# Longer rows for the slots of activations and split weights in a two-layer hybrid backbone kernel

## The chip, the core and the metric

The kernel runs on one core of one Trainium2 chip. The metric is device time in microseconds (us) from one launch, as the median of several executions. The times of the kernel before are 1237.31 us in the median of three (1236.67 to 1237.4). The profile shows one further execution, taken by the hardware profiler.

## The reference

Two consecutive layers (one gated-DeltaNet mixer, one HGRN2 mixer, each followed by a squared-ReLU MLP) are applied to 128 context tokens and 256 latent tokens that share one set of weights, with a model width of 1024. Cut to what matters for the time:

```python
for layer in range(2):
    sh1, sc1, gt1, sh2, sc2, gt2 = split(silu(c) @ w_ada[layer] + b_ada[layer], 6)
    h = rms_norm(x, g0) * (1 + sc1) + sh1
    mix = gated_deltanet(h) if layer == 0 else hgrn2(h)    # projections 1024 -> 4128 or 5120, back to 1024
    x = x + gt1 * rms_norm(mix, g1)
    h = rms_norm(x, g2) * (1 + sc2) + sh2
    x = x + gt2 * rms_norm(square(relu(h @ w1[layer])) @ w2[layer], g3)    # 1024 -> 4096 -> 1024
```

Everything is float32. The outputs are the 384 rows of x and the final states of both mixers.

## The kernel before

The 384 tokens are kept as three tiles of 128. All weights stream once from HBM. To multiply float32 numbers at one pass per matmul, each operand is split into a high and a low part of type fp32r: `hi` is a cast of the value (ScalarE), `lo` is value minus `hi` (VectorE), and a product becomes three matmuls, hi·hi, hi·lo and lo·hi (`mm3`). For weights, `split` makes the tiles `wh` and `wl` from a raw tile `wr` that a DMA has filled. For activations the split tiles are `hhi` and `hlo` (normalised input, transposed), and `mh` and `ml` (the hidden layer of the MLP).

A matmul with output `pj`, `k` or `nat` multiplies weights by `hhi`/`hlo`; `acc` is the output of the two down projections; `pf` holds the HGRN2 gate and value projections. In the names of the profile, the output stands first, then the moving operand (streamed, one column after the other) and the stationary one (loaded into the array by a LDWEIGHTS ahead of it), or the same two in the program's order.

All work tiles live in one pool that is divided into classes of equal slots, and a tile takes any free slot of its class. The classes that matter here:

- `L6`, 11 slots of 128 partitions by 6144 bytes (1536 float32): `hhi`, `hlo`, `mh`, `ml`, `xn`, `sg`, `hk`, `lhl`, and the Gated-DeltaNet tiles `PU`, `kT`, `T64`
- `wh` and `wl`, three slots each, 4096 bytes per partition
- `L1` (17 slots: `mr`, `cacc`, `cb`, `qT`, `CR` and others), `L3`, `L4` (`av`, `ar`, `hE`, `HC`, `x`), `Lh`, and `wr` (two slots of 8192 bytes)

In the program as it is built, the first byte of a slot within its partition, modulo 256, is called its phase here. Before the change every slot of `L6`, `wh` and `wl` has phase 96, since their rows are multiples of 256 bytes. `wr`, `L3`, `L4` and `Lh` have phase 224. The slots of `L1` are 1600 bytes apart and have phases 160, 224, 32 and 96 in turn. The constants have phases of their own (`sml` 128, `cst` 96). Within a tile, the pieces that a matmul reads begin at multiples of 512 bytes, so they keep the phase of the slot.

A planner (`Planner.run`) decides the order of all instructions and the slots from costs in a table; it doesn't look at addresses. `Planner.tile` registers a tile with its shape (L614 of the kernel before), `Planner.run` takes the real tile from the pool when its first instruction is issued (L798), and `fix` (L507) turns an access pattern of the planner into one of the real tile.

Of the kernel before, what the change touches and what calls it, by code (L numbers as in the profile page):

```python
# [10 lines left out]
B16 = mybir.dt.bfloat16  # L11
# [334 lines left out]
 'z:ld': 12621,  # L346
 'z:sp': 10349}
ZS = 2
DRY = False
V_KINDS = ((0, "gt2"), (1, "sh1"), (1, "sc1"), (1, "gt1"), (1, "sh2"), (1, "sc2"), (1, "gt2"))  # L350
ADA_KINDS = ("sh1", "sc1", "gt1", "sh2", "sc2", "gt2")
# [103 lines left out]
class VAP:  # L455
    def __init__(self, tensor, offset, ap, dtype, space):
        self.tensor, self.offset, self.ap, self.dtype, self.space = tensor, offset, ap, dtype, space
# [42 lines left out]


class VTile:
    def __init__(self, name):
        self.name, self.real = name, None


def fix(x):  # L507
    if isinstance(x, VAP):
        return bass.AP(tensor=x.tensor.real.tensor, offset=x.offset, ap=[list(d) for d in x.ap])
    return x  # L510


# [27 lines left out]
class Planner:  # L540
# [71 lines left out]
        return op  # L612

    def tile(self, pool, shape, dtype, cls, tag, bufs, space=None):  # L614
        t = VTile(f"{tag}_{len(self.tile_of)}")
        bufs = BUFS.get(tag, bufs)
        ap, st = [], 1
        for n in reversed(shape):
            ap.append((st, n))
            st *= n  # L620
        self.tile_of[t.name] = {"cls": cls, "tag": tag, "bufs": bufs, "first": None, "left": 0, "got": False, "name": t.name,
                                "make": (pool, shape, dtype), "v": t}
        return VAP(t, 0, ap[::-1], dtype, space)

    def run(self):
# [163 lines left out]
        self.plan = done  # L789
        if DRY:  # L790
            return
# [28 lines left out]
class Vec:  # L820
# [14 lines left out]
    def tensor_tensor(self, out, in0, in1, op):  # L835
        rate = 1.042 if self.e == "V" else (164.0 if op == ALU.pow else 2.1)
        base = None if self.e == "V" else (300.0 if op == ALU.pow else 150.0)
        self._go(lambda: self.r.tensor_tensor(fix(out), fix(in0), fix(in1), op), _n(out), [out], [in0, in1], rate, base=base)  # L838

    def scalar_tensor_tensor(self, out, in0, scalar, in1, op0, op1, accum_out=None):  # L840
        w = [out] if accum_out is None else [out, accum_out]
        kw = {} if accum_out is None else {"accum_out": accum_out}
        self._go(lambda: self.r.scalar_tensor_tensor(fix(out), fix(in0), fix(scalar), fix(in1), op0, op1, **{k: fix(v) for k, v in kw.items()}), _n(out), w,  # L843
                 [in0, scalar, in1], 1.042, extra=62.0 * (accum_out is not None), scal=(scalar,))

    def tensor_scalar(self, out, in0, s1, s2, op0, op1=None):
        rate = (0.521 if self._fast(out, in0) else 1.042) if self.e == "V" else 1.042
        args = (out, in0, s1, s2, op0) if op1 is None else (out, in0, s1, s2, op0, op1)
        self._go(lambda: self.r.tensor_scalar(*[fix(x) for x in args]), _n(out), [out], [in0, s1, s2], rate, base=None if self.e == "V" else 160.0, scal=(s1, s2))  # L849
# [95 lines left out]
def kernel(ctx: ExitStack, tc: tile.TileContext, a, o):  # L945
# [12 lines left out]
    def tl(cls, tag, bufs, shape, dtype=F):  # L958
        return pl.tile(pool, shape, dtype, cls, tag, bufs)
# [366 lines left out]
    def zgate(p):  # L1326
        t = tl("L1", "th", 2, [128, T])
        S.activation(t, p, AF.Tanh, scale=0.5)
        zs = tl("L1", "zs", ZS, [128, T])
        V.scalar_tensor_tensor(zs, t, 1.0, p, ALU.add, ALU.mult)  # L1330
# [14 lines left out]
    def gdn(oT):  # L1345
# [136 lines left out]
        def gate(h, p):  # L1482
            pl.unit(f"z{h}")
            zs = tl("L1", "zs", ZS, [128, T])
            S.activation(zs, p, AF.Silu)
# [599 lines left out]
```

## Time and profile before

| What | Value |
|---|---|
| median of 3 executions | 1237.31 us (1236.67 to 1237.4) |
| profiled execution, its own time | 1235.33 us |
| span of its trace, first to last instruction | 1233.3 us |
| mean granted TensorE clock, share of full speed | 0.966 |
| TensorE busy (PE) | 1180.0 us, 96% of the span |
| weight loads (PEld), beside the matmuls | 1047.6 us, 85% |
| VectorE busy (DVE) | 800.2 us, 65% |
| ScalarE busy (ACT) | 635.4 us, 52% |
| GpSimd busy (POOL) | 66.1 us, 5% |

PE's busy time is a union of intervals whose ends are modelled; one matmul's own duration overlaps the next one. What a matmul costs in a stream is therefore the time from one start to the next, which a merged piece of the chain of waits gives when it is divided by its count.

### The profile page before, as it was taken

The numbers are of one execution on the slowest core, as the hardware profiler recorded it, in microseconds if no ns is written. First come the engines' busy times: TensorE is split into PE (matmuls) and PEld (weight loads), VectorE is DVE, ScalarE is ACT, GpSimd is POOL, SyncE is SP. The second block draws the span as 40 slices with busy tenths as digits, with TensorE's granted clock in tenths as the row PEclk, the third lists the DMA queues.
The fourth block names the chain that finished last, engine by engine and source line by source line (L and its number), as shares of the span: only waits on it lengthen the run. The fifth ranks groups of instructions, "written<-read, shape, count | busy, mean of one in ns | idle before, by whom it ended". The sixth has DMA issues, their size and how long they took to land.

```text
span 1233.3 us, 20383 instructions
## 1 busy us (share of the span) xinstructions
PE 1180.0 (96%) x7936; PEld 1047.6 (85%) x7936; DVE 800.2 (65%) x1578; ACT 635.4 (52%) x1283; POOL 66.1 (5%) x156
## 2 busy tenths in 40 slices
PE   6998998999998999999998999999998999999997
PEld 3775988888987998989988998888986999888986
DVE  4484878867999986666539967767666542333334
ACT  3383464775646643343436567674655564333442
POOL 1111001000002000000002000000002000000000
PEclk9996996899998999999998999999999999999999
DMA  9868771675353875556436642233432334233432
GB/s 359 318 248 281 225 214 33 198 248 186 119 182 134 302 237 191 192 184 205 152 115 205 210 150 97 76 110 111 159 133 84 107 137 137 103 127 118 138 129 86
DMA packets 82642, 207.82 MB, mean 169 GB/s; under 512 B 26058, under 2 KB 47842, under 8 KB 70514
## 3 DMA queue, kind: packets, MB, share of 16 engines
q1 hardware_dynamic: 82546, 206.53, 49.4%
q8 instruction: 62, 1.02, 0.3%
q14 instruction: 34, 0.28, 0.1%
HBM read 192.52 MB, written 13.99 MB: 167 GB/s over the span
## 4 chain that ended last, share of the span: by engine, by line
PE 60%; DVE 7%; ACT 5%; issue 2%; POOL 1%; POOLq 0%; DVEq 0%; ACTq 0%
PE acc L924 24%; PE pj L924 21%; PE pf L924 7%; PE nat L924 3%; PE pb L924 2%; PE po L924 1%; DVE wl L838 1%; ACT L887 1%; DVE A L838 1%; POOL rstd L838 1%; PE pb L930 1%; PE pj L930 1%; ACT wh L892 1%; DVE avj L843 1%; DVE hQD L838 1%
## 5 line engine op out<-in xcount | busy, mean ns | idle before, releaser
L838 DVE TENSOR_TENSOR wl<-wr,wh 128x1024 fp32r<-128x1024 f32 (+2 forms) x228 | 266.6, 1171 | 268.1 <-ACT wh L892 260.1
L892 ACT CAST wh<-wr 128x1024 fp32r<-128x1024 f32 (+2 forms) x228 | 230.3, 1010 | 403.8 <-PE pj L924 178.0
L924 PE MATMUL pj<-hhi,wh 128*128 128x384 f32 x800 | 272.5, 343 | 0.0
L924 PE MATMUL pj<-hhi,wl 128*128 128x384 f32 x800 | 271.1, 342 | 0.0
L924 PE MATMUL pj<-hlo,wh 128*128 128x384 f32 x800 | 270.9, 341 | 0.0
L924 PEld LDWEIGHTS pj<-hhi,wh 128*128 128x128 f32 x800 | 151.6, 190 | 2.4 <-issue 0.8
L924 PEld LDWEIGHTS pj<-hlo,wh 128*128 128x128 f32 x800 | 151.5, 190 | 1.8 <-issue 0.4
L924 PEld LDWEIGHTS pj<-hhi,wl 128*128 128x128 f32 x800 | 151.6, 190 | 1.4 <-DVE wl L838 0.5
L924 PE MATMUL acc<-wl,mh 128*128 128x512 f32 x384 | 149.5, 390 | 0.0
L924 PE MATMUL acc<-wh,ml 128*128 128x512 f32 x384 | 149.3, 390 | 0.0
L924 PE MATMUL acc<-wh,mh 128*128 128x512 f32 x384 | 145.4, 390 | 0.0
L843 DVE SCALAR_TENSOR_TENSOR avj<-av,cvec 128x1024 bf16<-128x1024 f32 x112 | 135.5, 1218 | 6.9 <-DMA dd<-dec 3.7
L924 PEld LDWEIGHTS acc<-wl,mh 128*128 128x128 f32 x384 | 72.1, 188 | 15.8
L924 PEld LDWEIGHTS acc<-wh,mh 128*128 128x128 f32 x384 | 72.1, 188 | 14.7
L924 PEld LDWEIGHTS acc<-wh,ml 128*128 128x128 f32 x384 | 72.1, 188 | 14.2
L924 PE MATMUL pf<-wh,hhi 128*128 128x384 f32 x192 | 63.6, 346 | 2.3 <-ACT hhi L892 2.3
L924 PE MATMUL pf<-wl,hhi 128*128 128x384 f32 x192 | 63.9, 342 | 0.1
L924 PE MATMUL pf<-wh,hlo 128*128 128x384 f32 x192 | 63.8, 345 | 0.0
L843 DVE SCALAR_TENSOR_TENSOR cacc<-cb,sml,cacc 128x392 f32<-128x392 f32 x96 | 58.9, 619 | 5.4 <-ACT cacc L887 4.5
L887 ACT ACT_TABLE_LOAD x35 | 44.9, 1283 | 3.6 <-DVE hk L849 2.4
L838 DVE TENSOR_TENSOR ml<-mr,mh 128x384 fp32r<-128x384 f32 x56 | 30.2, 554 | 14.7 <-PE acc L924 7.5
L924 PEld LDWEIGHTS pf<-wh,hhi 128*128 128x128 f32 x192 | 36.2, 190 | 2.9 <-ACT hhi L892 2.5
(255 smaller groups left out, 1898.0 us busy)
## 6 DMA issues: line engine op xcount, KB each, us to landing
wr<-in_w_dram SPq DMA_DIRECT2D x64, 1024.0 KB
av<-in_wv_dram SPq DMA_DIRECT2D x56, 512.0 KB
ar<-in_wa_dram SPq DMA_DIRECT2D x40, 512.0 KB
wr<-in_gq_dram SPq DMA_DIRECT2D x14, 1024.0 KB
wr<-in_hfi_dram SPq DMA_DIRECT2D x16, 768.0 KB
wr<-in_hqz_dram SPq DMA_DIRECT2D x8, 1024.0 KB
wr<-in_gout_dram SPq DMA_DIRECT2D x4, 1024.0 KB
wr<-in_hout_dram SPq DMA_DIRECT2D x4, 1024.0 KB
```

The source lines that it names most:

```text
L838: self._go(lambda: self.r.tensor_tensor(fix(out), fix(in0), fix(in1), op), _n(out), [out], [in0, in1], rate, base=base)
L843: self._go(lambda: self.r.scalar_tensor_tensor(fix(out), fix(in0), fix(scalar), fix(in1), op0, op1, **{k: fix(v) for k, v in kw.items()}), ...
L887: self.pl.add("S", lambda: self.r.activation(fix(out), fix(in_), func, **{k: fix(v) for k, v in kw.items()}), cost, w, [x for x in (in_, b ...
L892: self.pl.add("S", lambda: self.r.copy(fix(out), fix(in_)), cost, [out], [in_])
L924: self.pl.add("PE", lambda: self.r.matmul(fix(out), lhsT=fix(lhsT), rhs=fix(rhs), start=start() if callable(start) else start, stop=stop, ...
L930: self.pl.add("PE", lambda: self.r.transpose(fix(out), fix(in_), fix(ident)), 111.0, [out], [in_, ident], geo=(4, 4))
```

## The change

Tiles of class `L6` now take slots of 1544 float32 (6176 bytes) and those of `wh` and `wl` slots of 1040 (4160 bytes). The tile in it is as large as before, and only the distance between slots grows, by 32 and by 64 bytes. `fix` puts the longer row into the partition step of the access pattern.

```diff
+ROW = {'L6': 1536 + 8, 'wh': 1024 + 16, 'wl': 1024 + 16}
...
 def fix(x):
     if isinstance(x, VAP):
-        return bass.AP(tensor=x.tensor.real.tensor, offset=x.offset, ap=[list(d) for d in x.ap])
+        t = x.tensor
+        p, f = divmod(x.offset, t.row)
+        dims = [list(d) for d in x.ap]
+        if t.wide != t.row:
+            assert dims[0][0] % t.row == 0
+            dims[0][0] = dims[0][0] // t.row * t.wide
+        return bass.AP(tensor=t.real.tensor, offset=p * t.wide + f, ap=dims)
     return x
...
     def tile(self, pool, shape, dtype, cls, tag, bufs, space=None):
-        t = VTile(f"{tag}_{len(self.tile_of)}")
+        row = 1
+        for n in shape[1:]:
+            row *= n
+        wide = ROW[cls] if cls in ROW and dtype != B16 else row
+        t = VTile(f"{tag}_{len(self.tile_of)}", row, wide)
+        if wide != row:
+            real_shape = [shape[0], wide]
+        else:
+            real_shape = shape
...
-                                "make": (pool, shape, dtype), "v": t}
+                                "make": (pool, real_shape, dtype), "v": t}
```

In the two programs as they are built, all five engines have the same instructions in the same order with the same waits; they differ in addresses alone. The phases after the change are 224, 0, 32, 64, 96, 128, 160, 192, 224, 0 and 32 for the eleven slots of `L6`, 192, 0 and 64 for `wh`, and 128, 192 and 0 for `wl`. `L1`, `L3`, `L4`, `Lh` and `wr` stay where they were. Each tile is in the slot of the same number as before. Instructions with at least one operand in a slot of `L6`, `wh` or `wl`: 5416 of 6676 matmuls of the program, 461 of ScalarE, 446 of VectorE, 4 of GpSimd, and 24 DMAs. The partition needs 736 bytes more and holds them.

## Rows read from the trace of the kernel before

**Rows 1.** The page: busy time of each engine.
```profile
PE 1180.0 (96%) x7936; PEld 1047.6 (85%) x7936; DVE 800.2 (65%) x1578; ACT 635.4 (52%) x1283; POOL 66.1 (5%) x156
```

**Rows 2.** The page: shares of the chain of waits, by engine.
```profile
PE 60%; DVE 7%; ACT 5%; issue 2%; POOL 1%; POOLq 0%; DVEq 0%; ACTq 0%
```

**Rows 3.** Busy time of each engine in five stretches.
```profile
core 0: us, PE busy (x) PEld busy (x) DVE busy (x) ACT busy (x) POOL busy (x), PEclk, DMA share, GB/s
0.00:300.00 300.00, 271.77 (x2270) 228.57 (x2270) 208.63 (x537) 164.42 (x394) 25.83 (x75) 0.90 0.70 232
300.00:421.00 121.00, 115.41 (x722) 106.26 (x722) 112.53 (x224) 72.42 (x188) 12.19 (x27) 0.97 0.50 175
421.00:649.00 228.00, 228.00 (x1141) 205.77 (x1141) 143.59 (x196) 95.72 (x138) 1.10 (x4) 1.00 0.56 188
```

**Rows 4.** The chain from 420 to 650 us: start, length, what.
```profile
420.81 33.31 PE pj L924 x192
454.12 32.68 PE acc L924 x144
486.80 16.66 PE pj L924 x96
...
618.86 31.26 PE acc L924 x138
```

**Rows 5.** Groups of PE by shape: one of each triple, and a load.
```profile
L924 PE MATMUL pj<-hhi,wh 128*128 128x384 f32 x800 | 272.5, 343 | 0.0
...
L924 PE MATMUL acc<-wh,mh 128*128 128x512 f32 x384 | 145.4, 390 | 0.0
...
L924 PE MATMUL pf<-wh,hhi 128*128 128x384 f32 x192 | 63.6, 346 | 2.3 <-ACT hhi L892 2.3
...
L924 PE MATMUL acc<-wh,hhi 128*128 128x512 f32 x96 | 38.0, 406 | 0.2 <-ACT hhi L892 0.2
...
L924 PE MATMUL nat<-wh,hhi 128*128 128x256 f32 x96 | 26.8, 292 | 3.4 <-ACT hhi L892 3.4
...
L924 PE MATMUL k<-hhi,wh 128*128 128x384 f32 x40 | 13.2, 361 | 0.2 <-ACT hhi L892 0.2
```

**Rows 6.** The timeline of PE at 785 us: start, length, what.
```profile
785.49 0.52 PE L924 MATMUL pb<-lhl,CR 128*128 128x256 f32 x3
785.84 1.31 PE L924 MATMUL pb<-HC,lhl 128*128 128x512 f32 x5
```

**Rows 7.** The timeline of PE at 454 us, first and eighth matmul of a piece.
```profile
453.96 0.39 PE L924 MATMUL acc<-wh,mh 128*128 128x512 f32 x1
...
455.57 0.40 PE L924 MATMUL acc<-wl,mh 128*128 128x512 f32 x1
```

**Rows 8.** The chain from 390 to 420 us, one piece.
```profile
395.81 5.67 PE nat L924 x47
```

**Rows 9.** Groups of DVE by shape: busy and mean ns, idle time before.
```profile
L838 DVE TENSOR_TENSOR wl<-wr,wh 128x1024 fp32r<-128x1024 f32 x188 | 229.7, 1223 | 252.3 <-ACT wh L892 244.4 <-PE pj L924 4.7
L843 DVE SCALAR_TENSOR_TENSOR cacc<-cb,sml,cacc 128x392 f32<-128x392 f32 x96 | 58.9, 619 | 5.4 <-ACT cacc L887 4.5
```

**Rows 10.** Tile mr on DVE, 420 to 660 us: minimum, median, maximum ns.
```profile
L838 DVE TENSOR_TENSOR ml<-mr,mh x25: 548/553/559, 422.4 to 621.3; 128x384 fp32r<-128x384 f32 x25
```

**Rows 11.** Groups of ACT by shape: busy and mean ns, idle time before.
```profile
L892 ACT CAST wh<-wr 128x1024 fp32r<-128x1024 f32 x188 | 197.7, 1051 | 354.2 <-PE pj L924 167.0 <-PE acc L924 166.2 <-PE pf L924 15.0
L892 ACT CAST mh<-mr 128x384 fp32r<-128x384 f32 x56 | 27.6, 512 | 1.2
```

**Rows 12.** DMA issues that touch L6: count and size of one.
```profile
du<-PU SPq DMA_DIRECT2D x8, 48.0 KB
...
T<-dt SPq DMA_DIRECT2D x8, 48.0 KB
PU<-dt SPq DMA_DIRECT2D x8, 48.0 KB
```

**Rows 13.** Tile T, 150 to 330 us: issue times of its DMAs.
```profile
L941 SPq DMA_DIRECT2D T<-dt x8: 422/468/5198, 169.3 to 234.3; - x8
```

More of the change, by code (lines that the diff above doesn't have):

```diff
@@ L502, with __init__ @@
 class VTile:
-    def __init__(self, name):
-        self.name, self.real = name, None
+    def __init__(self, name, row, wide):
+        self.name, self.real, self.row, self.wide = name, None, row, wide
 def fix(x):
     if isinstance(x, VAP):
-        return bass.AP(tensor=x.tensor.real.tensor, offset=x.offset, ap=[list(d) for d in x.ap])
+        t = x.tensor
[5 more added lines that the diff above has]
+        return bass.AP(tensor=t.real.tensor, offset=p * t.wide + f, ap=dims)
     return x
```

## The prediction

> **What bounds the kernel now.** I read the busy times first. TensorE is busy for 96% of the span, and no other engine comes near it [rows 1]. The chain of waits says the same with less weight: 60% of it is TensorE, 7% VectorE, 5% ScalarE [rows 2]. So the question is whether TensorE streams at its best rate or loses something that an address could give back or take away.
>
> The stretches answer where to look: from 421 to 649 us (the MLP of the first layer) TensorE is busy all the time, the granted clock is 1.00, and nothing else is near its limit [rows 3]. In that stretch the chain is nothing but matmuls [rows 4]. The piece of 192 matmuls of 384 columns takes 33.31 us, 173.5 ns from one start to the next. The piece of 144 with 512 columns takes 32.68 us, 226.9 ns. [...] What is left is 13 ns in both (173.5 - 384 x 0.417 and 226.9 - 512 x 0.417). The piece of 47 with 256 columns gives 120.6 ns, and again about 14 ns are left [rows 8]. So a matmul in a stream costs its columns at full clock and a constant of some 13 ns. All of these have both operands in slots of phase 96, the one case that the change removes. [...]
>
> **The change part by part.** No instruction, wait or order changes, so the sum has one term for each kind of access.
>
> *Matmuls.* The groups that read two re-placed slots hold 3 x (800 + 384 + 192 + 96 + 96 + 40) = 4824 matmuls [rows 5]. The bound on a gain is the whole constant, 4824 x 13.1 ns = 63 us. For the value itself I use the places where the trace of before already has unequal phases. In the HGRN2 stage a matmul streams `HC` (phase 224) while weights from `lhl` (phase 96) are loaded for the next one: five of 512 columns take 1.31 us, and with the last one's 0.39 us taken off, as in the group beside it, (1.31 - 0.39) / 4 = 230 ns [rows 6, 7]. Three of 256 columns that stream `lhl` (96) against weights in `CR` (160) start within 0.35 us of the next piece, 117 ns each [rows 6]. With 64 or 128 bytes between the phases the constant is thus still 10 to 16 ns. The other bound comes from the same rows: 230 is 3.1 ns more than 226.9, and 4824 x 3.1 ns = 15 us of loss. But matmuls with equal phases take 230 ns too when they come right after another shape: the eight from 453.96 to 455.57 us stand (455.57 - 453.96) / 7 = 230 ns apart [rows 7]. So I take 0, nearest to these rows, between -63 and +15 us.
>
> [...] Each matmul here has a weight load of its own, and no run here shows a stream without them.
>
> *VectorE and ScalarE.* The trace has these engines at many phases. The 25 subtractions `ml<-mr,mh` of the first MLP take 548 to 559 ns [rows 10], while `mr` sat in slots of phase 96 six times, 224 nine times, 32 eight times and 160 twice, and `mh` always at 96. So equal and unequal phases of the two inputs lie within 1%. The four taps of the convolution read `cb` shifted by 4, 8, 12 and 16 bytes against a `cacc` that stays, and have a mean of 619 ns over 96 instructions [rows 9]; 392 elements cost what 384 and 8 more would. The largest groups in re-placed slots are the subtraction into `wl` (229.7 us) and the casts into `wh` and `mh` (197.7 and 27.6 us) [rows 9, 11]. A change of 1% of the two engines' share is 4.6 us of busy time; only 12% of the chain is theirs [rows 2], which leaves about 0.5 us either way. I take 0.
>
> *DMAs.* Of 24 DMAs of 48 KB each, 8 read from `PU`, 8 write `T64` and 8 write `PU` [rows 12], all in pieces of 128 bytes. The issues of the 8 into `T64` have a median of 468 ns and a minimum of 422 ns [rows 13]. If an address shifted each by that difference, it would be 24 x 46 ns = 1.1 us either way, in a stretch in which TensorE still has other work for 272 of 300 us [rows 3]. I take 0. The large transfers go to `wr`, `L3` and `L4`, which don't move.
>
> The sum is 0. The profiled execution's own time is 1235.33 us (span 1233.3 us and 2.0 us around it), so its time after is 1235.3 us; it stands 2.0 us below the median of 1237.31, and so I predict 1237.3 us for the median.
>
> **The rivals.** *A: the constant is a collision.* The stream of one matmul and the weight load of the next walk through the same phase, the load takes cycles from the stream, and slots at unequal phases end that. For it speaks that loads are busy for 85% of the span beside the matmuls [rows 1]; against it that the constant is there at phase distances of 64 and 128 [rows 6]. About a tenth of the pairs would still meet at equal phases, so up to 57 us go; where TensorE is not the chain less arrives, at 60% [rows 2] 34 us. The time would be 1180 to 1203 us, and I name 1190 us. It decides from 0.5 ns per matmul (0.5 x 4824 = 2.4 us).
>
> *B, slower: unequal phases cost the stream.* If the 230 ns of `HC` are due to its phase and not to the change of shape, the 15 us come on top, 1252 us. It has the same point from which it decides, 0.5 ns. For it is the 230 against 226.9; against it are the equal phases with the same 230 [rows 7].
>
> *C: the clock.* Nothing that TensorE does changes by the sum, but a stretch at lower granted clock may come or go when events shift by nanoseconds. From 300 to 421 us the clock is 0.97 [rows 3]; one such loss is 0.03 x 121 = 3.6 us, to either side: 1233.7 or 1240.9 us.
>
> **How the numbers follow.** No change has 0.84, A 0.06, B 0.05, C 0.05, half to each side. About 0.2%, 2.5 us, is what a measurement can tell from no change. Faster by over 0.2% is A and half of C, 0.085; slower is B and half of C, 0.075; within it 0.84. The range needs only the first case: 1237.3 us with 1.6 us for the DMAs and the two engines and 1.7 us of the 2.0 us by which single executions of before stood apart, 1234.0 to 1240.6 us.
>
> **What would show it.** In the profile after, pieces of 384 columns should still come to 173.5 ns and of 512 to 226.9 ns, the group into `wl` to 1223 ns and the cast into `wh` to 1051 ns. A shows as a piece of 192 that takes well under 33.31 us, B as one that takes over 33.5 us. If these stay and the time moves, the granted clock or the DMAs of the inverse should show why. I am wrong if a phase distance that before doesn't have (32 bytes, or slots at a multiple of 64) behaves unlike those it has: in before nearly all slots are at odd multiples of 32, and so the trace can't exclude it.

## The result, and the profile after

| | before | after |
|---|---|---|
| median of four executions | 1236.99 us (1236.06 to 1237.4) | 1243.95 us (1243.58 to 1244.44) |
| profiled execution, its own time | 1235.33 us | 1243.92 us |
| span of its trace | 1233.3 us | 1242.0 us |
| mean granted TensorE clock | 0.966 | 0.967 |

The ratio is 1.0058 with an interval of [1.004, 1.0075]: slower by 0.6%, 3.35 us above the upper end of the predicted range. What comes next shows the kernel after, in which the same code stands 15 lines further down (the matmul's L924 is L939).

The page, busy time of each engine, stands against [rows 1]: PE has 10.5 us more for the same 7936 instructions, VectorE 0.9 us more, ScalarE 0.4 us.

```profile
PE 1190.5 (96%) x7936; PEld 1051.6 (85%) x7936; DVE 801.1 (65%) x1578; ACT 635.8 (51%) x1283; POOL 66.7 (5%) x156
```

The shares of the chain by engine are nearly those of [rows 2], so no new wait has come to the front.

```profile
PE 60%; DVE 7%; ACT 6%; issue 2%; POOL 2%; POOLq 0%; DVEq 0%; ACTq 0%
```

The windows over the first MLP (time, then busy us and count for each engine, granted clock, DMA share, GB/s) show PE busy throughout at a clock of 1.00, as in [rows 3]; the stretch has only become longer.

```profile
core 0: us, PE busy (x) PEld busy (x) DVE busy (x) ACT busy (x) POOL busy (x), PEclk, DMA share, GB/s
...
421.00:656.00 235.00, 235.00 (x1158) 209.41 (x1157) 146.85 (x199) 97.98 (x145) 2.01 (x7) 1.00 0.55 186
```

The chain of waits in that stretch (start, length, what) is where the loss can be seen:

```profile
422.18 33.61 PE pj L939 x192
455.79 33.43 PE acc L939 x144
489.22 16.80 PE pj L939 x96
506.02 16.66 PE acc L939 x72
522.68 16.81 PE pj L939 x96
539.49 33.55 PE acc L939 x144
573.04 16.79 PE pj L939 x96
589.83 16.72 PE acc L939 x72
606.55 16.83 PE pj L939 x96
623.38 31.90 PE acc L939 x138
```

It is the same row of pieces as in [rows 4], each a little longer. From the first one's start to the last one's end it was 229.31 us (650.12 - 420.81), and it is 233.10 us. Over the five acc pieces that is 5.1 ns for each of 570 matmuls of 512 columns (132.26 us against 129.35 us, the latter from the chain of run e1 below, whose pieces agree with [rows 4] to 0.01 us wherever both are shown), over the five pj pieces 1.5 ns for each of 576 matmuls of 384 columns (100.84 against 99.95 us). These two make the 3.80 us. Over the whole program the starts of the matmuls say the same: in the six groups of [rows 5], pairs of neighbours in one group that no pause parts stand 5.0 ns further apart in the MLP's acc (1152 matmuls) and 3.6 ns in the output projections (288). In pj it is 0.95 ns (2400), in pf and k 0.85 ns (696), and in nat -1.1 ns (288; between -0.4 and -1.5, by the gap that is taken as a pause). The sum is 9.3 us (5.8 + 1.0 + 2.3 + 0.6 - 0.3), against 8.7 us that the span has grown.

The rest of the prediction's rows stayed where they were. The groups of VectorE, ScalarE, tile `mr` and tile `T` (duration as mean, or as minimum, median, maximum) answer to [rows 9, 11, 10, 13]:

```profile
L853 DVE TENSOR_TENSOR wl<-wr,wh 128x1024 fp32r<-128x1024 f32 x188 | 229.9, 1224 | 259.1 <-ACT wh L907 253.7 <-PE pj L939 4.8
...
L858 DVE SCALAR_TENSOR_TENSOR cacc<-cb,sml,cacc 128x392 f32<-128x392 f32 x96 | 58.9, 620 | 5.5 <-ACT cacc L902 4.6
```

```profile
L907 ACT CAST wh<-wr 128x1024 fp32r<-128x1024 f32 x188 | 197.5, 1051 | 361.5 <-PE acc L939 171.3 <-PE pj L939 169.2 <-PE pf L939 15.1
```

```profile
L853 DVE TENSOR_TENSOR ml<-mr,mh x25: 551/555/561, 423.8 to 625.8; 128x384 fp32r<-128x384 f32 x25
```

```profile
L956 SPq DMA_DIRECT2D T<-dt x8: 422/468/5857, 170.2 to 234.6; - x8
```

1224 ns against 1223, 620 against 619, 1051 against 1051, a median of 555 against 553 and of 468 against 468: in these groups of VectorE, ScalarE and the DMAs no cost of the new addresses can be seen.

### The profile page after: what moved, and what is told of

The parts are those of the page before. It is cut to its first block, busy times and chain, and to the rows that moved or that the text cites. A ratio compares the mean times of both kernels' runs of the same rounds, so it can differ in the third digit from the quotient of the medians.

```text
span 1242.0 us, 20383 instructions
## 1 busy us (share of the span) xinstructions
PE 1190.5 (96%) x7936; PEld 1051.6 (85%) x7936; DVE 801.1 (65%) x1578; ACT 635.8 (51%) x1283; POOL 66.7 (5%) x156
## 4 chain that ended last, share of the span: by engine, by line
PE 60%; DVE 7%; ACT 6%; issue 2%; POOL 2%; POOLq 0%; DVEq 0%; ACTq 0%
PE acc L939 25%; PE pj L939 21%; PE pf L939 7%; PE nat L939 3%; PE pb L939 2%; PE po L939 1%; DVE wl L853 1%; ACT L902 1%; DVE A L853 1%; POOL rstd L853 1%; PE pb L945 1%; ACT wh L907 1%; DVE avj L858 1%; PE pj L945 1%; DVE hQD L853 1%
## 5 line engine op out<-in xcount | busy, mean ns | idle before, releaser
L939 PE MATMUL pj<-hhi,wh 128*128 128x384 f32 x800 | 274.1, 345 | 0.0
L939 PE MATMUL pj<-hhi,wl 128*128 128x384 f32 x800 | 272.9, 344 | 0.0
L939 PE MATMUL pj<-hlo,wh 128*128 128x384 f32 x800 | 272.5, 343 | 0.0
L939 PEld LDWEIGHTS pj<-hhi,wh 128*128 128x128 f32 x800 | 152.0, 190 | 2.5 <-issue 0.8
L939 PEld LDWEIGHTS pj<-hlo,wh 128*128 128x128 f32 x800 | 151.8, 190 | 1.8 <-issue 0.4
L939 PEld LDWEIGHTS pj<-hhi,wl 128*128 128x128 f32 x800 | 151.8, 190 | 1.4 <-DVE wl L853 0.5
L939 PE MATMUL acc<-wh,ml 128*128 128x512 f32 x384 | 151.2, 395 | 0.0
L939 PE MATMUL acc<-wl,mh 128*128 128x512 f32 x384 | 151.1, 394 | 0.0
L939 PE MATMUL acc<-wh,mh 128*128 128x512 f32 x384 | 147.1, 394 | 0.0
L939 PEld LDWEIGHTS acc<-wl,mh 128*128 128x128 f32 x384 | 72.1, 188 | 16.7
L939 PEld LDWEIGHTS acc<-wh,ml 128*128 128x128 f32 x384 | 72.1, 188 | 16.6
L939 PEld LDWEIGHTS acc<-wh,mh 128*128 128x128 f32 x384 | 72.1, 188 | 16.4
L939 PE MATMUL pf<-wh,hhi 128*128 128x384 f32 x192 | 63.1, 343 | 2.3 <-ACT hhi L907 2.3
L939 PE MATMUL pf<-wh,hlo 128*128 128x384 f32 x192 | 64.4, 348 | 0.0
L939 PE MATMUL pf<-wl,hhi 128*128 128x384 f32 x192 | 64.1, 342 | 0.0
L939 PE MATMUL acc<-wh,hhi 128*128 128x512 f32 x96 | 38.3, 409 | 0.2 <-ACT hhi L907 0.2
```

Source lines behind the costliest of these rows:

```text
L939: self.pl.add("PE", lambda: self.r.matmul(fix(out), lhsT=fix(lhsT), rhs=fix(rhs), start=start() if callable(start) else start, stop=stop, ...
```

## The experiments

**Two layouts of one source.** The start addresses of the slots follow from the order in which the classes take their first tile. For one instruction, which is the first to write both to an `L6` tile and to a small tile, `Planner.run` goes through `op.tiles` in the order that a Python set gives, and that differs from build to build. With the small tiles first, all slots of `L6`, `wh` and `wl` in the kernel before have phase 96: the equal layout, which was measured as before. With `L6` first, its slots have phase 224 and those of `wh` and `wl` 96, 128 bytes apart. The executions of the kernel before that ran beside the experiments took 1246.67 to 1247.62 us in the medians of their five groups, and all ratios below are to these. No trace of them exists. That they are the second layout is inferred from their time, which e2 meets with a ratio of 1.0003. So every experiment fixes the order with a sort, with the small tiles first where nothing else is said, and is read against e1 or e17 as well.

Theories: **D**, the difference of phase between the running stream and the weights loaded beside it decides; its rivals are that the absolute phase decides, that longer rows cost something by themselves, and that VectorE or ScalarE takes the cycles.

In the table a piece is the first of its kind in the chain after 420 us: 192 matmuls pj of 384 columns, 144 acc of 512. Times are medians in us with the range of the executions.

| run | phases of L6; wh; wl | time | ratio to the runs beside | pj x192 | acc x144 |
|---|---|---|---|---|---|
| e1, equal | 96; 96; 96 | 1237.62 (1235.87 to 1240.3) | 0.9923 [0.9905, 0.9941] | 33.30 | 32.68 |
| e17, equal again | 96; 96; 96 | 1238.15 (1236.48 to 1239.85) | 0.9932 [0.992, 0.9944] | 33.30 | 32.68 |
| e6 | 0; 0; 0 | 1239.17 (1234.97 to 1239.77) | 0.9933 [0.9917, 0.995] | 16.66 (x96) | 32.68 |
| e9, wh and wl 256 bytes on | 96; 96; 96 | 1237.7 (1235.93 to 1239.49) | 0.992 [0.9905, 0.9935] | 33.30 | 32.96, 32.68 |
| e5, longer rows | 96; 96; 96 | 1236.68 (1233.96 to 1239.62) | 0.9917 [0.9898, 0.9936] | 33.30 | 32.76 |
| e2, L6 first | 224; 96; 96 | 1247.61 (1245.7 to 1251.32) | 1.0003 [0.999, 1.0016] | 33.71 | 33.59 |
| e7 | 96; 128; 128 | 1243.05 (1242.46 to 1249.35) | 0.9967 [0.9954, 0.998] | 33.31 | 33.58 |
| e8 | 96; 160; 160 | 1242.24 (1237.86 to 1244.63) | 0.9954 [0.9934, 0.9975] | 33.29 | 32.96 |
| e11, after, L6 first | eight; 192, 0, 64; 128, 192, 0 | 1244.94 (1242.12 to 1246.52) | 0.9979 [0.9966, 0.9992] | 33.60 | 33.43 |
| e10, after, small first | as e11, L6 turned by 128 | 1244.0 (1241.69 to 1245.89) | 0.997 [0.996, 0.9981] | 33.59 | 33.47 |
| e3, rows of wh, wl | 96; 96, 160, 224; 32, 96, 160 | 1244.2 (1242.84 to 1251.23) | 0.9979 [0.9965, 0.9993] | 33.54 | 33.42 |
| e4, rows of L6 | eight; 192; 192 | 1246.45 (1243.92 to 1251.7) | 0.9994 [0.998, 1.0008] | 33.50 | 33.53 |
| e12 | low parts 64 on | 1239.6 (1237.98 to 1241.74) | 0.9939 [0.9921, 0.9957] | 32.89 | 33.30 |
| e13 | low parts 128 on | 1244.34 (1242.76 to 1245.71) | 0.9975 [0.9959, 0.9991] | 33.71 | 33.27 |
| e15 | hlo 64 on | 1238.12 (1236.85 to 1239.39) | 0.9933 [0.9921, 0.9945] | 33.39 | 32.68 |
| e16 | wl 64 on, not at 512 | 1237.42 (1236.7 to 1241.52) | 0.9927 [0.9915, 0.9938] | 33.56 | 32.66 |
| e14 | hlo and wl 64 on, not at 512 | 1231.97 (1230.47 to 1234.46) | 0.9885 [0.9869, 0.99] | 32.89 | 32.66 |

For e6 a piece of 96 stands (16.66 us in e1 too), since its first one is cut at another place.

### e1 and e2: the two layouts of the kernel before

```diff
-                for t in op.tiles:
+                for t in sorted(op.tiles, key=lambda t: t["cls"] == "L6"):   # e1, small tiles first
+                for t in sorted(op.tiles, key=lambda t: t["cls"] != "L6"):   # e2, L6 first
```

> The kernel before, with the order of the classes in SBUF fixed (the small tiles, then L6, wh, wl), so that every slot of L6, wh and wl has phase 96. Theory D (distance): what costs TensorE is a distance other than 0, modulo 256 bytes, between the row that a matmul streams and the weights that are loaded beside it. Theory A (absolute): what costs is a start at a multiple of 64 bytes. Theory S (spread): what costs is that slots of one class differ among themselves. All three expect the time of before, 1237 us +- 1.5, and 33.3 us for the piece of 192 matmuls of 384 columns, if the kernel before was laid out like this on the chip. Where it was laid out with L6 first, D expects a difference here.

> The kernel before with L6 laid out ahead of the small tiles: all slots of L6 at phase 224, all of wh and wl at 96, so each matmul of the projections has distance 128 to the weights loaded beside it. D: slower than the equal layout. From after's excess over before (33.61 - 33.31 us per 192 of 384 columns, 33.43 - 32.68 us per 144 of 512 columns) 1.6 ns x 3384 + 5.2 ns x 1440 = 13 us in all, of which about 7 to 13 us reach the end: 1244 to 1250 us. A and S: 1237 us +- 1.5, since no slot starts at a multiple of 64 and no class is spread.

The chain of e1:

```profile
421.62 33.30 PE pj L924 x192
454.92 32.68 PE acc L924 x144
487.60 16.66 PE pj L924 x96
504.27 16.36 PE acc L924 x72
520.63 16.66 PE pj L924 x96
537.29 32.68 PE acc L924 x144
569.98 16.66 PE pj L924 x96
586.64 16.36 PE acc L924 x72
603.00 16.66 PE pj L924 x96
619.67 31.27 PE acc L924 x138
```

The chain of e2:

```profile
422.93 33.71 PE pj L924 x192
456.64 33.59 PE acc L924 x144
```

e1 repeats the pieces and the time of the kernel before. e2 has the same instructions in the same order, and 10 us more (1247.61 against 1237.62): 6.3 ns for each matmul in the acc piece ((33.59 - 32.68) / 144), 2.1 ns in the pj piece. Phases alone cost this, with no longer row anywhere. In e2 the starts of 512-column matmuls during which neither VectorE nor ScalarE was busy lie 232.9 ns apart, and those with both busy 232.8 ns. So neither of the two takes the cycles. DMAs are out in the same way: where no DMA packet was under way, the starts in e2 stand 232.8 ns apart (501 pairs), and with twelve or more under way 232.9 ns (444 pairs). GpSimd was busy for 0.2 us of the stretch from 421 to 650 us, and no PSUM address differs between the programs as they are built. What is left are TensorE's own reads, the moving rows and the weights. That these two collide is the explanation left over; no trace shows the collision itself.

### e6 and e9: is it the absolute phase, and is 256 bytes the period?

```diff
+GAP = {'L6': 40}   # e6: 40 float32 left free ahead of L6;  e9: {'wh': 64}
...
+                    if t["cls"] in GAP and t["cls"] not in gaps:
+                        gaps.add(t["cls"])
+                        pool.tile([128, GAP[t["cls"]]], F, tag="gap" + t["cls"], bufs=1, name="gap" + t["cls"])
```

> Small tiles first, 160 bytes left free ahead of L6: every slot of L6, wh and wl at phase 0, all distances 0, all starts at multiples of 64; wr stays at 224. D (distance between the streamed row and the load): the equal layout again, 1237.5 us +- 2, pieces of 33.3 and 32.7 us. A (start at a multiple of 64): the 512-column matmuls carry 5 ns or more, 1440 x 5 ns = 7 us, 1244 us or more. N (nearness to what VectorE, ScalarE and DMAs use, wr at 224): also other than 1237, since the distance to wr changes from 128 to 224.

> Small tiles first, L6 at 96, 256 bytes left free ahead of wh: all phases modulo 256 equal as in the equal layout, but the distance between streamed row and load is an odd multiple of 256. D with a period of 256 bytes: 1237.5 us +- 2, pieces of 33.3 and 32.7 us. D with a longer period (512 or more): slower, 1242 to 1250 us.

Both run as e1 does: 1239.17 and 1237.7 us. Moving all three classes to phase 0 changes nothing, and neither do 256 bytes between activations and weights. In e9 the first acc piece has 32.96 us, but all later ones are those of e1; what the first one caught is open.

### e7 and e8: 32 and 64 bytes between activations and weights

```diff
+GAP = {'wh': 8}    # e7: 32 bytes;  e8: {'wh': 16}, 64 bytes
```

> Small tiles first, L6 at 96, and 32 bytes left free ahead of wh: all of wh and wl at 128, distance +32 where L6 is streamed and -32 where wh or wl is streamed. D: slower by 5 to 13 us, 1242 to 1250 us. A: wh and wl start at multiples of 64, L6 doesn't; the 512-column matmuls stream wh and wl and carry about 5 ns each, 1440 x 5.2 ns = 7.5 us: 1244 us. S: 1237 us +- 1.5.

> Small tiles first, L6 at 96, 64 bytes left free ahead of wh: all of wh and wl at 160, distance +64 and -64, no start at a multiple of 64. D: slower by 5 to 13 us, 1242 to 1250 us. A and S: 1237 us +- 1.5.

The chain of e7:

```profile
421.47 33.31 PE pj L929 x192
454.78 33.58 PE acc L929 x144
```

The chain of e8:

```profile
422.83 33.29 PE pj L929 x192
456.12 32.96 PE acc L929 x144
```

In these pieces the 512-column matmuls lose 6.3 ns at 32 bytes and 1.9 ns at 64 bytes. Over all 1132 pairs of neighbours in the acc of both MLPs it is 5.7 and 1.7 ns, and 5.3 ns at the 128 bytes of e2. The 384-column ones lose nothing at 32 or 64 bytes, though they lose 2.1 ns at 128 bytes in e2. The price depends on the distance and on the length of the stream together, not in a simple order of either. There is a rival to the length: in acc the weights are streamed and the activations loaded, in pj it is the other way round. The matmuls of pf, which stream weights with 384 columns, speak against it: their starts stand 173.9 ns apart in e7, 173.5 in e8 and 175.9 in e2, against 174.1 in e1, so they behave like pj (173.7, 174.1 and 175.9, against 173.9) and not like acc.

### e10, e11, e3, e4: the change again, in both layouts and in parts

```diff
+                for t in sorted(op.tiles, key=lambda t: t["cls"] != "L6"):   # e11; e10 with ==, both on the changed kernel
-ROW = {'L6': 1536 + 8, 'wh': 1024 + 16, 'wl': 1024 + 16}
+ROW = {'wh': 1024 + 16, 'wl': 1024 + 16}   # e3, small tiles first
+ROW = {'L6': 1536 + 8}                     # e4, small tiles first
```

> The changed kernel with the small tiles laid out first: L6 at 96, 128, 160, ... , wh at 192, 0, 64, wl at 128, 192, 0. D: distances of all sizes, so on average a part of what 32 to 128 bytes cost: 1241 to 1248 us. The changed kernel was measured at 1243.95; if it was laid out like this, its pieces of 33.61 us (192 of 384 columns) and 33.43 us (144 of 512) come back to 0.02 us.

> The changed kernel with L6 laid out first: L6 at 224, 0, 32, ..., wh and wl as in the run beside it. D: 1241 to 1248 us, and another division over the pieces than with the small tiles first. If the changed kernel was laid out like this when it was measured, its pieces of 33.61 and 33.43 us come back to 0.02 us and the time to 1244 us +- 2.

> One part of the change alone: longer rows for wh and wl, L6 with its old rows at phase 96, small tiles first; wh at 96, 160, 224 and wl at 32, 96, 160. Distances of 0, 64, 128 and 192, a quarter of the pairs equal. Theory D (the distance, modulo 256 bytes, between the streamed row and the load beside it): between the equal layout (1237.6) and the changed kernel (1244 to 1245): 1239 to 1243 us.

> The other part alone: longer rows for L6, wh and wl with their old rows at one phase (192), small tiles first; L6 at 96, 128, 160, ... Distances of all multiples of 32 and few equal pairs. D: 1242 to 1246 us. A theory by which wh and wl alone matter expects 1237.6 us.

The chain of e11:

```profile
423.38 33.60 PE pj L939 x192
456.99 33.43 PE acc L939 x144
490.42 16.80 PE pj L939 x96
```

The chain of e3:

```profile
423.98 33.54 PE pj L939 x192
457.52 33.42 PE acc L939 x144
```

e11 repeats the measured kernel after piece by piece (33.61, 33.43, 16.80), so the order of classes was that one. Against the layout with `L6` first the same change is faster, 0.9979 [0.9966, 0.9992]; against the equal one it is slower by 6 to 7 us. What it does is to replace one distance for all by a mixture of distances, which costs 5.1 ns a matmul in the acc pieces of the first MLP and 3.6 ns in the output projections. Each part alone does the same: longer rows of the weights 1244.2 us, longer rows of the activations 1246.45 us. They don't add up: either alone breaks the equality of phases. Both came out a little over what D had led me to expect, e3 over 1239 to 1243 us and e4 over 1242 to 1246 us.

### e5: longer rows, equal phases

```diff
-ROW = {'L6': 1536 + 8, 'wh': 1024 + 16, 'wl': 1024 + 16}
+ROW = {'L6': 1536 + 64, 'wh': 1024 + 64, 'wl': 1024 + 64}
+                for t in sorted(op.tiles, key=lambda t: t["cls"] == "L6"):
```

> The changed kernel with rows longer by 256 bytes in L6, wh and wl, small tiles laid out first, so that every slot has phase 96 again. If the phases alone cost the time: 192 matmuls of 384 columns in 33.30 us, 144 of 512 in 32.68 us, 1237 to 1238 us. If the longer rows themselves (partition step, gaps between slots) cost something: as the changed kernel, 33.6 and 33.4 us, 1244 us.

The chain of e5:

```profile
421.14 33.30 PE pj L939 x192
454.44 32.76 PE acc L939 x144
487.20 16.66 PE pj L939 x96
503.87 16.36 PE acc L939 x72
```

1236.68 us: with rows longer by 256 bytes, and the phases of e1, nothing is lost. The longer row and its partition step cost nothing that can be seen; with equal phases the whole loss is gone.

### e12 and e13: only the low parts moved

```diff
+GAP = {'wl': 16}                   # e13: 32
+ROW = {'L6': 1536 + 64}
+STEP = {'hlo': 16, 'ml': 16}       # e13: 32; tiles of these names begin so many float32 further in their slot
...
+        self.step = STEP.get(name.rsplit('_', 1)[0], 0)
...
-        return bass.AP(tensor=t.real.tensor, offset=p * t.wide + f, ap=dims)
+        return bass.AP(tensor=t.real.tensor, offset=p * t.wide + f + t.step, ap=dims)
```

High parts stay at 96, low parts lie at 160 (e13: 224). In the order of `mm3` the running stream and the next weights are always both high or both low, so their distance is 0 throughout.

> A layout chosen by D: all distances 0, but high and low parts at different phases: hhi, mh and wh at 96, hlo, ml and wl at 160, so that the stream beside which a weight load runs always has its phase, and consecutive streams differ by 64 bytes. D alone: as the equal layout, 1237.5 us +- 2, pieces of 33.3 and 32.7 us. From the two places in the spread layouts that are of this kind (matmul triples with hi 192, lo 0 and hi 64, lo 128, both with equal distances: 1.0 to 1.7 ns less per matmul of 384 columns than in the equal layout): 33.3 - 192 x 1.4 ns = 33.03 us for the piece, and 3384 x 1.4 ns = 4.7 us in all, of which about 3 arrive: 1234.5 us.

> As the paired layout, with the low parts 128 bytes beyond the high ones (96 and 224): all distances 0. D alone: 1237.5 us +- 2, pieces of 33.3 and 32.7 us. If it matters that a stream and the weights loaded two matmuls on, or the stream before it, differ: other than that, by up to 2.5 ns per matmul to either side, 1231 to 1246 us.

The chain of e12:

```profile
421.58 32.89 PE pj L946 x192
454.47 33.30 PE acc L946 x144
487.77 16.46 PE pj L946 x96
```

The chain of e13:

```profile
424.54 33.71 PE pj L946 x192
458.25 33.27 PE acc L946 x144
```

D falls here in its simple form. With the distance 0 everywhere, 512-column matmuls still lose about 4 ns (33.30 and 33.27 against 32.68 us). And 384-column ones do something no other run had shown: with 64 bytes they *gain* 2.1 ns each (32.89 against 33.30 us), with 128 they lose 2.1 ns. The step from the high to the low part counts as well. The gain that I had hoped for in e12 as a whole, 1234.5 us, didn't come, since the acc matmuls lost what the pj matmuls won.

### e14 to e17: which step, and a version faster than both

```diff
+ROW = {'L6': 1536 + 64, 'wl': 1024 + 64}
...
+        lo.tensor.step = 16 if shape[-1] != 512 else 0   # in split: e14, e16
...
-    def new_hT():
+    def new_hT(step=16):                                 # e14, e15
...
+        for t in lo:
+            t.tensor.step = step
...
+        new_hT(0)                                        # in out_proj
```

> All slots equal at phase 96, and in the stages of 384 and 256 columns alone the low parts (hlo outside the two output projections, wl of other shapes than 512 columns) begin 64 bytes further, at 160, as they did in the run with low parts 64 bytes ahead of high parts. If what counts is the number of columns together with the step between high and low part: 192 matmuls of 384 columns in 32.89 us as there, 144 of 512 in 32.68 us as with equal phases; the gain at 384 is 1.6 ns x 3 x (800 + 192 + 40 + 96) = 5.4 us of matmul time, of which 60 to 90% arrive: 1233 to 1235 us, against 1237.6 with equal phases. Rival: the 384 gain was tied to the 512 part of that kernel (for instance clock or queue), 33.30 and 1237.6 us.

> Only hlo 64 bytes further (outside the output projections), wh and wl and everything else at phase 96. If two streams that follow one another decide (hhi, then hlo): 192 matmuls of 384 columns in 32.9 us, 1233 to 1235 us. If the load of the next weights against the running stream decides (now one in three at a distance of 64, measured 0.2 ns dearer): 33.31 us, 1237.6 us.

> Only wl of the 384 and 256 column stages 64 bytes further; hlo, hhi, wh at phase 96. If two streams that follow one another decide: 33.30 us for 192 of 384 columns in pj (streams all at 96), 1237 us. If the step from one load to the next decides: 32.9 us, 1233 to 1235 us. If neither alone does, but stream and load must step together: 33.3 to 33.4 us in both this run and the one with hlo alone.

> The equal layout once more, for comparison on the same chip: 1237.6 us within 2 us, 192 matmuls of 384 columns in 33.30 us, 144 of 512 in 32.68 us, by every theory.

The chain of e14:

```profile
421.63 32.89 PE pj L939 x192
454.52 32.66 PE acc L939 x144
487.19 16.43 PE pj L939 x96
503.62 16.34 PE acc L939 x72
```

The chain of e15:

```profile
421.46 33.39 PE pj L939 x192
454.84 32.68 PE acc L939 x144
```

The chain of e16:

```profile
424.21 33.56 PE pj L939 x192
457.77 32.66 PE acc L939 x144
```

Moving `hlo` alone costs 0.5 ns a matmul, moving `wl` alone 1.4 ns, moving both gains 2.1 ns. So neither two streams in a row nor two loads in a row decide by themselves: stream and load have to step together, which is what is left of D. The two parts alone cost more than I had expected: for wl alone at most 33.4 us if both must step, and it took 33.56. In e14 the gain isn't spread evenly over the three matmuls of `mm3`: from the first (streams `hhi`) to the second (streams `hlo`) the starts are 3.5 ns closer than in e17, the other two steps about 1 ns each. Nor is it the same in all groups of 384 columns: over the whole program it is 1.8 ns in pj (172.1 against 173.9 ns), 0.6 ns in pf (173.2 against 173.8) and nothing in k (173.95 against 174.0).

e14 leaves out the step for the 512-column matmuls, which lost by it, and takes 1231.97 us, a little less than the expected 1233 to 1235. Its four executions all lie below the fastest of e17, which ran beside it on the same chip (1230.47 to 1234.46 against 1236.48 to 1239.85), and the intervals of the two ratios don't meet. It is faster than the kernel before in either layout and than the kernel after: 0.5% under the one (1231.97 / 1238.15 = 0.995), 1.2% under the other (0.9885 [0.9869, 0.99]).

## Why the prediction was wrong

**What bounds the kernel** was right: TensorE's stream, and all of the time came from it (9.3 us by the starts of its matmuls, against 8.7 us that the span has grown).

**The matmul term** is the step that failed. It was taken as 0 between -63 and +15 us, and measured 9.3 us. The +15 us were there, worked out from the 230 ns of `HC`, and were dismissed, because equal phases also had 230 ns right after another shape. That observation was true, but it could decide nothing. In the trace of before, acc matmuls that follow a switch of shape stand 2.6, 5.3, 7.6 and 1.4 ns over 226.9 ns at the first four steps and 0.1 ns from the thirteenth on. The `HC` groups have at most five matmuls and so are all switch: 5.3 ns over 37 pairs, against about 4.5 ns that the first four steps of acc give. Neither a price nor its absence could be read there, and the after trace says the same, with the `HC` group hardly changed against [rows 6]:

```profile
790.93 0.52 PE L939 MATMUL pb<-lhl,CR 128*128 128x256 f32 x3
791.29 1.30 PE L939 MATMUL pb<-HC,lhl 128*128 128x512 f32 x5
```

The trace of before had no long stream of 384 or 512 columns at unequal phases at all, and the term was unknown between its bounds. The right conclusion from that was a wide range with a large weight on the loss. I gave that 0.05 and left it out of the range. The other bound, 63 us of gain, took the whole 13.1 ns that stand over a line through the two pieces of [rows 4] (32.68 / 144 - 33.31 / 192 = 53.45 ns over 128 columns, 0.4176 ns a column). That a gain could reach this and no more was my estimate, and no run shows it; the largest gain that a run showed in a long stream is 2.1 ns a matmul (e12, e14).

**The price per column**, 0.417 ns, I took as free of any cost of the phases. That was my estimate; the rows of before give no long stream at unequal phases to hold it against. What the runs show is a comparison: from the piece of 384 columns to that of 512 a matmul takes 53.5 ns more in e1 (226.9 - 173.4) and 57.7 ns more in e2 (233.3 - 175.6). Of these two layouts the equal one is the cheaper at both lengths. The kernel before had it, and the change gave it up.

**Rival B** had the right mechanism: unequal phases cost the stream, about 3.1 ns on each of 4824 matmuls, 1252 us. Measured are 5.0 ns on 1152, 3.6 on 288 and about 0.9 on 3096, and the 288 of 256 columns gained. The size for all at once was too large, since 384 columns mostly escape. Its marker, a piece of 192 over 33.5 us, came out at 33.61 us.

**Rival A** was wrong for this change: apart from 1.1 ns at 256 columns, no part of the 13 ns went. But e14 shows that less than the 173.5 ns is possible: 171.3 ns for 384 columns (32.89 / 192), 2.1 ns under the 173.4 ns of e17 (33.30 / 192), and 6.2 us in the whole program (1231.97 against 1238.15 us). No run here streams without a load per matmul, so how much of the 13 ns comes with the loads was not shown. **Rival C** did not take part: the clock has 0.967 against 0.966.

**VectorE, ScalarE and DMAs** at 0 were right, as the rows after show.

What I said would make me wrong, "a phase distance that before doesn't have behaves unlike those it has", named the place, but not the reason: also the distance 128, which before had only in short groups, costs 5 to 6 ns in a long stream of 512 columns (e2).

**What stays open:** whether reads of TensorE meet, which, and where. The runs show that the phases decide (1237.62 us in e1, 1247.61 us in e2), that 256 bytes more between activations and weights count for next to nothing (1237.7 us in e9), and that the gain of e14 needs stream and load to step together (32.89 us for the first pj piece, against 33.39 us with `hlo` alone in e15 and 33.56 us with `wl` alone in e16). They don't show why 384 columns gain from 64 bytes between high and low parts where 512 lose 4 ns, why pj gains more than pf, nor whether anything finer than 32 bytes matters.

## What to carry to other kernels

Where a long stream of matmuls each loads its own weights, the start of both tiles modulo 256 bytes was worth 1 to 3% of the matmul time here (2.1 of 173.4 ns, 6.3 of 226.9 ns). Keep moving rows and weights at equal phases. Where operands are split into high and low parts, try low parts 64 bytes further on both sides, and measure it for each length of stream: here it paid at 384 columns and cost 4 ns a matmul at 512. Fix the layout before a comparison: if a set or a hash decides the order of allocation, two builds of one source can differ by more than the change (here 10 us between e1 and e2, and 7 us for the change). A trace bounds a cost only with the pattern at issue; a few matmuls after a switch said nothing about a long stream here (up to 7.6 ns over 226.9 ns at the first four steps, 0.1 ns from the thirteenth on).

## What was not expected of the hardware

- The same 7936 matmuls in the same order take 10 us more (1247.61 against 1237.62 us) when the activations lie 128 bytes apart from the weights modulo 256.
- 512-column matmuls lose 5 to 6 ns at distances of 32 and 128 bytes (e7, e2) and 1.7 to 1.9 ns at 64 (e8); 384-column ones lose 2.1 ns at 128 and nothing at 32 and 64 (33.31 and 33.29 us for 192, against 33.30 us in e1).
- In the trace of before, acc matmuls right after a switch of shape stand up to 7.6 ns more than 226.9 ns apart (at the third step), at equal phases, and this fades to 0.1 ns from the thirteenth step on.
- A 64-byte step from high to low parts that stream and load make together brought the 384-column matmuls of the first MLP's pj from 173.4 to 171.3 ns each (e14).
